# An FFN entry dealt out by granule, squares of the norms summed on GpSimd, decay floors computed in the first mixer

## The chip, the cores and the metric

The kernel runs on one core of a Trainium2 chip. The metric is the time of one execution on the device, in microseconds, lower is better. A core has five engines with a queue of instructions each: TensorE (PE in the profile, with its weight loads as PEld), VectorE (DVE), ScalarE (ACT), GpSimd (POOL) and SyncE (SP), which here issues most of the DMAs. Each engine works off its queue in order. An instruction waits until the ones that it depends on, on other engines, have signalled, and everything behind it in its queue waits with it.

## The reference

A trunk of two layers on x of 512 tokens by 1024 features, all in float32. Each layer has three sub-layers, each with a norm ahead and a residual sum behind:

```python
x = x + 1/2 * SwiGLU_a(RMSNorm(x))          # FFN1
h = RMSNorm(x) @ W_mix_in                   # one projection for three token mixers
y = concat[shortconv | HGRN2 | FoX]
x = x + y @ W_mix_out
x = x + 1/2 * SwiGLU_b(RMSNorm(x))          # FFN2
# rms_norm(x) = x * rsqrt(mean(x*x) + 1e-6) * gain
# swiglu(h)   = (silu(gate) * up) @ w_out,  [gate | up] = h @ w_in,  2816 hidden features
```

HGRN2 is a recurrence with decay; the lower bound of its decay ("floor") comes from a softmax and a cumulative sum over a table of 2 x 256 logits, which depends on nothing else.

## The kernel before, in words

x is held transposed, features on the partitions: eight tiles of 128 features x 512 tokens (`xT`). TensorE multiplies in float32 to full precision with three passes: each operand is split into a rounded high part `hi` and the rest `lo`, and hi·hi, hi·lo and lo·hi are summed (`mm3`, L322, matmuls at L327, L333, L334). So every weight needs a cast on ScalarE (hi) and a subtraction on VectorE (lo): `parted` for plain weights (L315, L316), `prepare` for the halved products (L696, L698). Both share three buffers (tag `hl`); a buffer comes free when the matmuls on it are done.

An FFN has 22 tiles of 128 hidden features, each with a gate and an up part. Its first matmuls can't wait for the norm, which needs all of x; so the first tiles are **covered**: they are multiplied from x times the gain, without the norm's factor `inv`, and corrected afterwards. Four tiles are covered in three of the FFNs, six in the first (the opening of the program). Two tiles make a pass, indexed by f, of four **granules**; one granule is two blocks of 128 rows of the weights (a load on SP of 2 x 256 KB, a cast, a subtraction, 24 matmuls of 128x512). So an entry has 8 granules, the opening 12.

The remaining tiles use a Strassen-like scheme: each pair of tiles is made of seven **products** P1, P2, P6, P5, P7, P3, P4, in this order, of half the contraction and half the tokens each (24 matmuls of 128x256 each). Their operands on the side of x come from the normalised x in four quarters (a, b): a is the half of the features, b the half of the tokens. `halves_of_x` (L578) computes the quarters with `inv` (L594, four instructions each), the four totals of quarters (L600), and the seven operands, each with a cast on ScalarE and a rest on VectorE (`two`, L624). On the weights' side `halved` (L636) loads four quarters of 512 KB (L749 for the first pair, L667 later), and sums them on VectorE (`total`, L684) or by accumulating DMAs that GpSimd issues (L671, L714). The seven results are collected in PSUM banks and copied out: P1, P6, P7 and P4 accumulate in turn in one bank, so that P6 waits for the copy g1 (L789) and P7 for the copy g2 (L796); P3 accumulates in P5's bank behind the copy u2 (L799). Weights are prepared three products ahead (LEAD).

What makes the order: the framework's scheduler places instructions by priority, except for those that `follow` (L276) chains, which stay in the order in which the program issues them on their engine. Before, the products' own work is chained; of the entry only the last pass's clearing is (below); the granules' casts and rests run at high priority, and the operands are placed by the scheduler.

**The norm.** While x's tiles are completed, `norm_part` writes hi and lo of x times gain, squares the tile on ScalarE (L414, buffer tag g2 with two buffers in an FFN, t with more in the mixers) and adds it to `sqacc` on VectorE (L415): seven adds for each of the six norms. `end_norm` sums over the partitions with a matmul against a constant matrix (L427), then takes Ln and Exp on ScalarE (behind a load of their table, L263) and one Newton step (`rsqrt`: Square on ScalarE, three operations on VectorE, L421 to L423) to get `inv`.

**Clearing.** `finish` takes a covered tile from its two banks: gate and up times `inv` (L554, L555), Silu (L270), and two hidden products of 128x256 (L573, L576). In passes before the last this follows the pass; for the last pass the first tile is finished after the first product and the second after the third.

**In the opening** x is loaded in pieces and transposed on TensorE (L1509), constants are built, and `lower_bounds` (L835) computes the decay floors: some 20 small operations on VectorE, two on ScalarE and a load of the logits.

Of the kernel before, what the change touches and what calls it, by code (L numbers as in the profile page):

```python
# [23 lines left out]
P = 128  # L24
T = 512
# [11 lines left out]
LEAD = 3  # L37

# [124 lines left out]
class Trunk:  # L163
# [119 lines left out]
    def granule(self, parts, kk, ahead=True, skew=0):  # L283
# [14 lines left out]
        with self.tc.high_priority() if ahead else ExitStack():  # L298
            hi, lo = self.parted(st[:, : kk * c], 1 if ahead else kk, skew)
# [3 lines left out]
    def parted(self, src, pieces=1, skew=0):  # L303
# [38 lines left out]
    def stream_steps(self, jobs, parts_of, act, nk, mid=None, pre=None):  # L342
# [10 lines left out]
        while k < nk:  # L353
# [6 lines left out]
            rows = self.granule(parts_of(k, kk), kk, pre is None, skew)  # L360
# [6 lines left out]
            for n, ((acc, cols, toks, *more), j) in enumerate(order):  # L367
                if pre is not None and n == len(order) // 2:
                    pre(k, True)
                if isinstance(mid, tuple) and (k, len(order) // 2) == (mid[0], n):  # L370
                    mid[1]()
# [3 lines left out]
                if toks is None:  # L375
                    self.mm3(acc, hi[:, cols], lo[:, cols], ah, al, first, last)
# [15 lines left out]
    def norm_part(self, j, pool, xj=None, part=None):  # L392
# [19 lines left out]
        else:  # L412
            sq = pool.tile([P, T], F32, tag=self.tt, name=self.n("sq"), bufs=self.tb)
            nc.scalar.activation(sq, xj, AF.Square)  # L414
            nc.vector.tensor_add(self.sqacc, self.sqacc, sq)  # L415

    def rsqrt(self, out, v, r, t):

        nc = self.nc
        self.act(t, r, AF.Square)  # L420
        nc.vector.scalar_tensor_tensor(out=t, in0=v, scalar=EPS, in1=t, op0=ALU.add, op1=ALU.mult)  # L421
        nc.vector.tensor_scalar(t, t, scalar1=-0.5, scalar2=1.5, op0=ALU.mult, op1=ALU.add)
        nc.vector.tensor_mul(out, r, t)  # L423

    def end_norm(self, bank, pool):
        nc = self.nc
        nc.tensor.matmul(bank, self.ones_mean, self.sqacc, start=True, stop=True)  # L427
# [3 lines left out]
        self.act(r, bank, AF.Ln, bias=self.epsc)  # L431
        self.act(r, r, AF.Exp, scale=-0.5)
        self.inv = self.res.tile([P, T], F32, tag="inv", name=self.n("inv"))
        self.rsqrt(self.inv, bank, r, t)


    def ffn(self, w_in, w_out, next_gain, covered, begin=None, out=None):
# [5 lines left out]
        with tc.tile_pool(name=self.n("ffn"), bufs=1) as fp:  # L443
            self.tt, self.tb = "g2", 2
            if begin is not None:
                x, gain, logits = begin
            self.hq = {}
            halved = self.halved(fp, w_in, w_out, covered)
            finish = self.cover(fp, w_in, covered, begin, halved)
            for n, _ in enumerate(halved):  # L450

                if n in (1, 3):
                    finish(n // 2)
# [42 lines left out]
    def cover(self, fp, w_in, covered, begin, then):  # L496

# [4 lines left out]
        if begin is not None:  # L502
            x, gain, logits = begin
        for f in range(0, covered, 2):
# [6 lines left out]
            opening = f == 0  # L511

            def norm():
                self.end_norm(self.bank("pt" if self.ntog % 2 == 0 else "po"), fp)
                self.xparts = self.halves_of_x(fp)

                for _ in range(2 if begin is not None else 7):
                    next(self.xparts)

# [3 lines left out]
                parts, self.xact, KD,  # L523
                (2, norm) if opening and begin is None else None,
                (lambda *a: self.open_x(x, gain, fp, *a)) if opening and begin else None,
            )
            if opening and begin is not None:
                nt = iter(["xh4", "xl4", "xh5", "xl5", "xh6", "xl6", "r2", "r3", "r4", "r5"])
                self.build_consts(lambda dt: fp.tile([P, T], dt, tag=next(nt), name=self.n("c")))
                self.lower_bounds(logits, fp.tile([P, T], F32, tag="g1", name=self.n("lb"), bufs=2))  # L530
                norm()
            if f == 2:
                for _ in self.xparts:
                    pass
            if f + 4 == covered or f + 2 == covered:
                next(then)
            if opening:
# [1025 lines left out]
```

## Time and profile before

| | us |
|---|---|
| median of 3 runs | 1864.13 (1862.87 to 1872.72) |
| profiled execution | 1866.59 |
| span of it in the trace | 1864.7 |
| PE busy | 1834.3 (98%) |
| DVE busy | 1482.1 (79%) |
| ACT busy | 1009.1 (54%) |
| POOL busy | 177.4 (10%) |

The mean clock that TensorE was granted is 0.996 of full speed. Roughly, by the trace: the first FFN runs to 347 us, the first mixer to 605, its FFN2's first granule starts at 605 and its first product at 649; the second layer's FFN1 starts at 939 with its first product at 983, its FFN2 at 1522 with the first product at 1567. A row of a timeline is: start, duration, engine, line, operation, out<-in with shapes, and in brackets how long the engine stood idle before and what released it. A row of the waits has the waiting engine and group, what it waited for, and total us, times, longest. A row of a group has the count, busy us, mean ns of one, and the idle time before. A row of a stretch has its length, the busy time and count of the engine, the granted clock (PEclk), the share of the DMA engines and GB/s.

### The profile page before, as it was taken

Reading aid. Unit: us, or ns where it says so; the run is one execution under the profiler, and the core shown is the slowest. Engines: PE = TensorE matmul, PEld = TensorE weight load, DVE = VectorE, ACT = ScalarE, POOL = GpSimd, SP = SyncE. Lnnn points to the kernel's source line nnn. Section 1 sums busy time; section 2 is a strip of 40 time slices with the busy share of each in tenths; the row PEclk is TensorE's granted clock in tenths of the full one; section 3 lists DMA queues with packets and bytes.
Section 4 is the critical chain, followed back from the end, with each engine's and each line's share of the span. In section 5 each row is a group of like instructions: output and inputs, shape, how many; then the busy total and the mean of one; then the engine's idle time right before and its main releaser. Section 6 shows DMA issues by size and latency. Waiting matters only on the chain.

```text
span 1864.7 us, 33370 instructions
## 1 busy us (share of the span) xinstructions
PE 1834.3 (98%) x13528; PEld 1705.3 (91%) x13528; DVE 1482.1 (79%) x2101; ACT 1009.1 (54%) x1467; POOL 177.4 (10%) x182
## 2 busy tenths in 40 slices
PE   8999999999999999999999999999999999999999
PEld 6899999899878799999989999988998787999997
DVE  7889886678887978879687887967868878888883
ACT  4455554564666545555454555545547654555552
POOL 0011120100000011112001111201000000021210
PEclk9999999999999999999999999999999999999999
DMA  7658783232222757878265797813323237577662
GB/s 203 169 119 191 180 180 92 71 94 70 74 79 92 218 109 168 188 178 170 74 198 133 162 193 181 170 63 92 79 60 90 80 106 205 143 158 198 148 136 91
DMA packets 245418, 251.91 MB, mean 135 GB/s; under 512 B 19568, under 2 KB 230000, under 8 KB 245264
## 3 DMA queue, kind: packets, MB, share of 16 engines
q1 hardware_dynamic: 191664, 183.69, 32.9%
q0 software_dynamic: 53600, 66.09, 22.2%
q8 instruction: 106, 1.74, 0.4%
q14 instruction: 48, 0.39, 0.1%
HBM read 223.98 MB, written 2.10 MB: 121 GB/s over the span
## 4 chain that ended last, share of the span: by engine, by line
PE 85%; DVE 8%; ACT 3%; issue 2%; DMA 2%; SPq 0%; ACTq 0%; DVEq 0%
PE mm L327 12%; PE mm L334 12%; PE mm L333 12%; PE sc L334 6%; PE sc L327 6%; PE sc L333 6%; PE pt L327 6%; PE pt L333 6%; PE pt L334 6%; PE po L327 3%; PE po L334 3%; PE po L333 3%; DVE hl L316 1%; ACT hl L315 1%; PE po L1412 1%
## 5 line engine op out<-in xcount | busy, mean ns | idle before, releaser
L696 ACT CAST hl<-w 128x1024 fp32r<-128x1024 f32 x322 | 337.4, 1049 | 337.2 <-PE mm L334 76.6
L698 DVE TENSOR_TENSOR hl<-w,hl 128x1024 fp32r<-128x1024 f32 x322 | 393.0, 1222 | 102.5 <-ACT hl L696 102.5
L316 DVE TENSOR_TENSOR hl<-st,hl 128x512 fp32r<-128x512 f32 (+2 forms) x196 | 166.7, 852 | 117.0 <-ACT hl L315 115.9
L315 ACT CAST hl<-st 128x512 fp32r<-128x512 f32 (+2 forms) x196 | 146.6, 750 | 189.0 <-PE mm L334 66.9
L327 PE MATMUL mm<-xc,hl 128*128 128x256 f32 (+1 forms) x730 | 201.4, 276 | 1.1 <-ACT g L796 1.1
L334 PE MATMUL mm<-xc,hl 128*128 128x256 f32 x728 | 201.3, 276 | 0.0
L333 PE MATMUL mm<-xc,hl 128*128 128x256 f32 x728 | 201.2, 276 | 0.0
L334 PE MATMUL sc<-xc,hl 128*128 128x256 f32 x528 | 148.6, 281 | 8.7 <-DVE hl L698 8.7
L327 PE MATMUL sc<-xc,hl 128*128 128x256 f32 (+1 forms) x530 | 148.3, 281 | 0.9 <-ACT g L796 0.9
L333 PE MATMUL sc<-xc,hl 128*128 128x256 f32 x528 | 148.0, 280 | 0.0
L327 PEld LDWEIGHTS mm<-xc,hl 128*128 128x128 f32 x730 | 137.0, 188 | 1.6 <-ACT g L796 1.5
L333 PEld LDWEIGHTS mm<-xc,hl 128*128 128x128 f32 x728 | 136.7, 188 | 0.0
L334 PEld LDWEIGHTS mm<-xc,hl 128*128 128x128 f32 x728 | 136.6, 188 | 0.1
L327 PE MATMUL pt<-xc,hl 128*128 128x256 f32 x480 | 132.6, 276 | 0.0
L333 PE MATMUL pt<-xc,hl 128*128 128x256 f32 x480 | 132.6, 276 | 0.0
L334 PE MATMUL pt<-xc,hl 128*128 128x256 f32 x480 | 132.6, 276 | 0.0
L327 PE MATMUL mm<-hl,x 128*128 128x256 f32 (+1 forms) x384 | 112.6, 293 | 0.7 <-DVE ft L421 0.4
L334 PEld LDWEIGHTS sc<-xc,hl 128*128 128x128 f32 x528 | 101.3, 192 | 9.2 <-DVE hl L698 9.1
L327 PE MATMUL mm<-x,hl 128*128 128x512 f32 x272 | 109.6, 403 | 0.0
L334 PE MATMUL mm<-hl,x 128*128 128x256 f32 (+1 forms) x384 | 107.7, 281 | 0.0
L333 PE MATMUL mm<-hl,x 128*128 128x256 f32 (+1 forms) x384 | 107.5, 280 | 0.0
L334 PE MATMUL mm<-x,hl 128*128 128x512 f32 x272 | 106.5, 392 | 0.0
(470 smaller groups left out, 5693.3 us busy)
## 6 DMA issues: line engine op xcount, KB each, us to landing
w<-in_ffn_w_in_dram SPq DMA_DIRECT2D x140, 512.0 KB, 5.3
w<-in_ffn_w_out_dram SPq DMA_DIRECT2D x64, 512.0 KB, 4.4
w<-in_ffn_w_out_dram POOLq DMA_DIRECT2D x56, 512.0 KB, 9.1
st<-in_w_mix_in_dram SPq DMA_DIRECT2D x88, 256.0 KB, 2.7
st<-in_ffn_w_in_dram SPq DMA_DIRECT2D x72, 256.0 KB, 3.3
w<-in_ffn_w_in_dram POOLq DMA_DIRECT2D x35, 512.0 KB, 8.2
w<-S POOLq DMA_DIRECT2D x35, 512.0 KB, 4.7
st<-in_ffn_w_out_dram SPq DMA_DIRECT2D x24, 512.0 KB, 3.7
```

The lines of the kernel that those rows point to most:

```text
L315: a = nc.scalar.copy(hi, src[:, c : c + w])
L316: b = nc.vector.tensor_sub(lo, src[:, c : c + w], hi)
L327: i = nc.tensor.matmul(acc[:, c], ah, bh[:, c], start=first and c.start == 0, stop=False, skip_group_check=True,)
L333: nc.tensor.matmul(acc, ah, bl, start=False, stop=False, skip_group_check=True)
L334: i = nc.tensor.matmul(acc, al, bh, start=False, stop=last, skip_group_check=True)
L696: A(nc.scalar.copy(hi, src))
L698: return lambda: V(nc.vector.tensor_sub(lo, src, hi))
L1412: nc.tensor.matmul(self.ob[:, t0 + u * P : t0 + 2 * P], V[:, j, h % 4].rearrange("p a d -> p (a d)"), part[:, j, u:, :].rearrange("p i t - ...
```

## The change

Four things, in one diff:

1. A table `ENTRY` says for each granule (counted from 0; each half of a granule can be named; from twice the number of covered tiles on, the numbers count products) what is dealt there: the sum of squares over the partitions ("squares"), the rest of the norm ("norm"), a normalised quarter ("x a b"), a total of quarters ("+ a b c d": quarter (a, b) += quarter (c, d)), an operand ("P1"), the first total of weights ("sum"), the correction and Silu of a tile ("clear t") and its hidden products ("values t"). `deal` issues them, and chains all of them. `finish` and `halves_of_x` are gone. The granules of an entry are chained too and lose their high priority. With four covered tiles the norm's sum stands at 2.5 granules; it stood at 1.5 in the second layer's FFN1 and at 3 in the FFN2s. All operands except P3 and P4 and the first two tiles stand ahead of the first product, the rest between the products. The loads of the first products' weights (`halved`) are issued with the entry's first pass done.
2. The adds of `norm_part` go from VectorE to GpSimd.
3. `ngain` (minus the gain) is computed on VectorE instead of ScalarE.
4. `lower_bounds` is called in the first layer's mixer, behind the norm of its input.

In the queues as the changed kernel is built, the operand P4 and the total "0 0 += 1 0" stand on both engines ahead of the copy g2 that product P7 waits for, and on SP the four loads of the first products in FFN2 stand ahead of granule 4's loads, where they stood behind granule 6's.

```diff
+ENTRY = {
+    4: {
+        2.5: "squares", 5: "norm, x 0 0", 6: "P1, x 1 0", 7: "x 0 1, + 0 0 0 1, P2", 8: "P5, x 1 1",
+        9: "clear 0, + 0 0 1 1", 10: "P6, sum, clear 1, values 0, values 1, + 0 1 1 1, P7",
+        11: "P3", 12: "clear 2, values 2, + 0 0 1 0, P4", 14: "clear 3, values 3",
+    },
+    6: {
+        7: "norm, x 0 0", 8: "x 1 0, clear 0, clear 1", 9: "x 0 1, P1, + 0 0 0 1",
+        10: "P2, values 0, values 1, x 1 1", 11: "P5, clear 2, + 0 0 1 1", 12: "P6, values 2, sum, clear 3",
+        13: "values 3, + 0 1 1 1, P7", 14: "P3", 15: "+ 0 0 1 0, P4", 16: "clear 4, values 4",
+        18: "clear 5, values 5",
+    },
+}
...
-        with self.tc.high_priority() if ahead else ExitStack():
-            hi, lo = self.parted(st[:, : kk * c], 1 if ahead else kk, skew)
+        with self.tc.high_priority() if ahead and not keep else ExitStack():
+            hi, lo = self.parted(st[:, : kk * c], 1 if ahead else kk, skew, keep)
...
-            if pieces > 1:
+            if pieces > 1 or keep:
                 self.follow("a", a)
                 self.follow("v", b)
...
+            if deal is not None:
+                deal(k)
...
-                if isinstance(mid, tuple) and (k, len(order) // 2) == (mid[0], n):
-                    mid[1]()
+                if deal is not None and n == len(order) // 2:
+                    deal(k + 1)
...
             nc.scalar.activation(sq, xj, AF.Square)
-            nc.vector.tensor_add(self.sqacc, self.sqacc, sq)
+            nc.gpsimd.tensor_add(self.sqacc, self.sqacc, sq)
...
+        def clear(t):
+            gi = fp.tile([P, T], F32, tag="g2", name=self.n("gi"), bufs=2)
+            ui = fp.tile([P, T], F32, tag="u2", name=self.n("ui"), bufs=2)
+            pg, pu = tiles[t]
+            V(nc.vector.tensor_mul(gi, pg, self.inv))
+            V(nc.vector.tensor_mul(ui, pu, self.inv))
+            A(self.act(gi, gi, AF.Silu))
+            values[t] = gi, ui
+
+        def deal(n):
+            for what in filter(None, ENTRY[covered].get(n, "").split(", ")):
+                name, *at = what.split()
+                at = [int(v) if v.isdigit() else v for v in at]
+                if what == "squares":
+                    squares()
+                elif name == "norm":
+                    for e, i in self.take_norm(norm[0], fp):
+                        self.follow(e, i)
+                    self.table(SILU)
+                    self.signs()
+                elif name == "x":
+                    self.normalise(fp, *at)
+                elif name == "+":
+                    x, y = (self.xn[tuple(v)] for v in (at[:2], at[2:]))
+                    V(nc.vector.tensor_add(x, x, y))
...
+                else:
+                    self.operand(fp, name)
...
+            if f + 4 == covered:
+                next(halved)
+        for _ in halved:
+            pass
...
-        yield
-        total(u, "S2")
-        for s in seq[: LEAD - 1]:
-            prepare(*s)()
-        run(-1)
-        yield
-        prepare(*seq[LEAD - 1])()
+        for n, s in enumerate(seq[:LEAD]):
+            deal(2 * covered + n)
+            prepare(*s)()
+        run(-1)
...
             run(n)
-            yield
+            deal(2 * covered + LEAD + n)
...
                 bz = features([(H_F, 256)], ("mm", "mm"), lambda: self.end_norm(self.bank("pt"), hp))
+                if l == 0:
+                    self.lower_bounds(logits, hp.tile([P, T], F32, tag="t", name=self.n("lb"), bufs=8))
                 bg = features([(H_G, 256)], ("mm", "po"))
```

More of the change, by code (lines that the diff above doesn't have):

```diff
@@ L280, in follow, with granule @@
         self.chain[engine] = i.ins.name
[L283 removed]
+    def granule(self, parts, kk, ahead=True, skew=0, keep=False):
         nc = self.nc
@@ L445, in ffn @@
             if begin is not None:
-                x, gain, logits = begin
+                x, gain = begin
             self.hq = {}
[L448 to L453, printed above, removed]
+            self.cover(fp, w_in, w_out, covered, begin)
             f0, nf = CHUNKS[-1]
@@ L509, in parts @@
                 return [w_in[r, f * P : (f + 2) * P], w_in[r, FF + f * P : FF + (f + 2) * P]]
[L511 to L518, printed above, removed]
+            opening = f == 0 and begin is not None
             self.stream(
                 [(bk, slice(c, c + P), None) for bk, c in zip(banks, (0, 256, 128, 384))],
-                parts, self.xact, KD,
-                (2, norm) if opening and begin is None else None,
-                (lambda *a: self.open_x(x, gain, fp, *a)) if opening and begin else None,
-            )
@@ L532, in cover @@
[L532 to L537, printed above, removed]
[L538 to L559 removed]
+                squares()
```

153 lines of the change are left out of this document (77 added, 76 removed).

## The prediction

> **What bounds the kernel now.** I read first the page's busy shares, then what TensorE waits for, then the rows around its longest wait, then the groups by shape. Head of the page:
>
> ```profile
> span 1864.7 us, 33370 instructions
> PE 1834.3 (98%) x13528; PEld 1705.3 (91%) x13528; DVE 1482.1 (79%) x2101; ACT 1009.1 (54%) x1467; POOL 177.4 (10%) x182
> ```
>
> TensorE is busy for 98% of the span, so only a stall of TensorE, or its clock, can change the time. Its waits (total us, times, longest us):
>
> ```profile
> PE sc L334 <- DVE hl L698: 8.7, 2, 4.4
> PE mm L1509 <- DMA xs<-in_x_dram: 7.0, 2, 3.9
> ...
> PE po L327 <- DVE nt L421: 1.4, 1, 1.4
> PE mm L327 <- ACT g L796: 1.1, 2, 0.5
> PE sc L327 <- DVE gi L554: 1.1, 1, 1.1
> PE sc L327 <- ACT g L796: 0.9, 2, 0.5
> ```
>
> The change can reach all but the second (the load of x). The largest, 4.4 us, comes once in each FFN2, at the first halved product (TensorE's rows: start, duration):
>
> ```profile
> 649.47 0.33 PE L327 MATMUL sc<-xc,hl 128*128 128x128 f32 x2
> 649.64 0.33 PE L333 MATMUL sc<-xc,hl 128*128 128x256 f32 x1
> 654.33 0.58 PE L334 MATMUL sc<-xc,hl 128*128 128x256 f32 x1 [4.36 <-DVE hl L698]
> ```
>
> From issue to issue that is 4.7 us, 4.6 over the cadence. By stretches (length, PE busy, PEclk, DMA), the clock falls behind it:
>
> ```profile
> 645.00:650.00 5.00, 4.97 (x24) 1.00 0.38 112
> 650.00:655.00 5.00, 0.68 (x3) 0.70 0.66 210
> 655.00:660.00 5.00, 5.00 (x30) 0.62 0.58 105
> 660.00:665.00 5.00, 5.00 (x46) 1.00 0.72 105
> ```
>
> A clock of 0.70 over 5 us is 3.0 us at half clock, of which 0.7 us lie behind 654.33; 0.62 is 3.8 us more. So 6.8 us at half clock, 4.5 of them in work: 2.2 us lost. An FFN2 entry therefore loses 4.6 + 2.2, 0.5 at a later product (L796), and about 0.35 at the norm's sum (next fence): 7.6 us.
>
> ```profile
>   DVE sqa L415: 0.7, 2
> ```
>
> **The change, part by part.** The prices (group, busy, mean ns):
>
> ```profile
> L698 DVE TENSOR_TENSOR hl<-w,hl 128x1024 fp32r<-128x1024 f32 x322 | 393.0, 1222 | 102.5 <-ACT hl L696 102.5
> L684 DVE TENSOR_TENSOR w<-S,w 128x1024 f32<-128x1024 f32 x35 | 42.7, 1219 | 0.0
> L415 DVE TENSOR_TENSOR sqa<-sqa,sq 128x512 f32<-128x512 f32 x42 | 28.8, 685 | 0.0
> L600 DVE TENSOR_TENSOR xn<-xn,xn 128x1024 f32<-128x1024 f32 x16 | 19.3, 1220 | 0.0
> L634 DVE TENSOR_TENSOR xc<-xn,xc 128x1024 fp32r<-128x1024 f32 x16 | 19.1, 1220 | 0.0
> L573 DVE SCALAR_TENSOR_TENSOR hq<-gi,ui 128x256 f32<-128x256 f32 x18 | 7.6, 420 | 0.6 <-ACT gi L270 0.5
> L696 ACT CAST hl<-w 128x1024 fp32r<-128x1024 f32 x322 | 337.4, 1049 | 337.2 <-PE mm L334 76.6 <-PE pt L334 65.2 <-PE sc L334 58.2
> L270 ACT ACTIVATE gi<-gi 128x512 f32<-128x512 f32 x18 | 11.4, 632 | 15.1 <-DVE gi L554 15.1
> L796 ACT ACTIVATE g<-mm 128x512 f32<-128x512 f32 x13 | 7.7, 589 | 0.0
> ```
>
> Back to back they start closer together, as these rows of VectorE show:
>
> ```profile
> 643.63 0.69 DVE L554 TENSOR_TENSOR gi<-sc,inv 128x512 f32<-128x512 f32 x1
> 644.23 1.22 DVE L630 SCALAR_TENSOR_TENSOR xc<-xn,xc 128x1024 fp32r<-128x1024 f32 x1
> 645.37 1.22 DVE L634 TENSOR_TENSOR xc<-xn,xc 128x1024 fp32r<-128x1024 f32 x1
> ```
>
> So a 1024-column operation of VectorE occupies 1.14 us, a 512-column one 0.60; two hidden products of 256, 0.68. TensorE's clockwork shows in two casts that wait for the ends of granules 6 and 7 of the third FFN (rows of ScalarE):
>
> ```profile
> 977.78 1.05 ACT L696 CAST hl<-w 128x1024 fp32r<-128x1024 f32 x1 [0.53 <-PE pt L334]
> 983.22 1.05 ACT L696 CAST hl<-S 128x1024 fp32r<-128x1024 f32 x1 [4.39 <-PE pt L334]
> ```
>
> A granule lasts 983.22 − 977.78 = 5.44 us; a product, the same 24 matmuls on half the columns, 2.72.
>
> *The entry with four covered tiles (both FFN2s, second layer's FFN1).* The table takes the second tiles' clearing and hidden products from between the operands, so VectorE reaches the first product's weights early and the 4.6 us stall goes. What is late next is read from the queues as the changed kernel is built. The second product's weights (P2) use the buffer of granule 6, so their cast can't start before its end; everything in the given order stands behind them. I add from that end. Cast of P2's weights 1.05; on VectorE in this order: rest of P2's weights, operand P6, total S, clear of tile 1 (2 × 0.60), values of tiles 0 and 1 (2 × 0.68), addition 0 1 += 1 1, operand P7, weights of P6 and P5, total S3, operand P3, g1's subtraction (0.60), weights of P7, clear of tile 2 (1.20), values 2 (0.68), addition 0 0 += 1 0. Of these, eleven have 1024 columns (the rests of four weights, three operands, two totals, two additions): 11 × 1.14 = 12.5. Operand P7 waits for its own cast behind the addition, 1.05 + 0.15 = 1.2; values 2 wait for their Silu, 0.8. On ScalarE operand P4's cast follows that last addition (1.0), then P3's weights (0.95), and only then the copy g2 (0.6), which the fifth product, P7, needs because it accumulates into g2's bank. With 0.2 for the ends: 1.05 + 12.5 + 2.4 + 2.04 + 1.2 + 0.6 + 0.8 + 1.0 + 0.95 + 0.6 + 0.2 = 23.3 us. P7 is due after granule 7 and four products, 5.44 + 4 × 2.72 = 16.3. **TensorE stalls 7.0 us in each such entry**, about 1.1 at P6 (g1's copy stands behind operand P7's cast) and 5.9 at P7. Before, P4's operand was done ahead of the products and this copy was only 0.5 late. A 5.9 us idle is longer than the one behind which half clock lasted 6.8 us. That began about 2.4 us into the idle; so 3.5 us of it fall into the idle, 3.3 into work: 1.6 us lost.
>
> Second layer's FFN1: 7.0 + 1.6 − 0.5 (row L796 mm) = **+8.1**. Each FFN2: 7.0 + 1.6 − 7.6 = +1.0, **+2.0** in both.
>
> *The entry with six tiles (opening).* The norm's end stood behind the floors' logarithm on ScalarE, which leaves:
>
> ```profile
> 41.93 0.20 ACT L270 ACTIVATE lb<-lb 128x4 f32<-128x4 f32 x1 [3.05 <-DVE lb L885]
> ```
>
> It moves ahead by these 3 us, and f=0's banks are cleared at granule 8: the waits on nt and gi, 1.6 + 1.2 with what TensorE lost around them, go. But the addition 0 0 += 1 0 (1.14) and P4's operand (1.05 + 0.1 for its cast, 1.14) now stand between S3 and g1's subtraction, on the chain from the first product's end to g2's copy:
>
> ```profile
> 86.37 1.05 ACT L696 CAST hl<-w 128x1024 fp32r<-128x1024 f32 x1 [1.79 <-PE mm L334]
> 87.32 0.59 ACT L789 ACTIVATE g<-mm 128x512 f32<-128x512 f32 x1
> ...
> 94.34 0.58 ACT L796 ACTIVATE g<-mm 128x512 f32<-128x512 f32 x1
> ```
>
> It was 0.5 late (8.5 us from the cast at 86.37) and becomes 3.4 longer: a stall of 3.9. Stalls: −2.8 + 3.4 = +0.6. 3.9 is nearer to the 4.6 that cost clock than to the 1.4 and 1.1 that didn't; I take 2.0 for it: **+2.6**, ends −2.8 and +3.
>
> *Squares on GpSimd.* 42 adds of 0.685 us leave VectorE (28.8 us). The trace has no elementwise add on GpSimd. Its 182 instructions average 177.4 / 182 = 1.0 us, VectorE's add takes 0.69: I take 1.0 (it is GpSimd's own), ends 0.69 and 2.2, the latter over three times VectorE's. With two square buffers in an FFN, ScalarE's next square waits for the add before last. In the mixers the sum has room:
>
> ```profile
> 351.71 0.69 DVE L415 TENSOR_TENSOR sqa<-sqa,sq 128x512 f32<-128x512 f32 x1
> ...
> 354.93 1.02 PE L427 MATMUL pt<-sqa,ones_mean 128*128 128x512 f32 x2
> ```
>
> 2.5 us between. In FFN2 the last add at 1.0 comes before its sum (which also moves to 2.5 granules; in the second layer's FFN1 that is 5.4 us later, hidden by the clearing dealt behind it). Adds of 1.0 cost nothing; at 2.2 the Squares hold up the casts of the entry: +6 us in each FFN2. In the opening the adds stand on GpSimd behind an accumulating DMA (first row), but the last square ends at 34.3 (second) and the sum follows at 35.83, 1.5 later:
>
> ```profile
> 16.92 1.44 POOL L671 DMA_DIRECT2D w<-in_ffn_w_in_dram  x1 [15.27 <-DMA w<-in_ffn_w_in_dram]
> ```
>
> ```profile
> 33.73 0.60 ACT L414 ACTIVATE sq<-po 128x512 f32<-128x512 f32 x1 [2.34 <-DVE xT L1498]
> ```
>
> ```profile
> 35.83 1.06 PE L427 MATMUL po<-sqa,ones_mean 128*128 128x512 f32 x2
> ```
>
> So 1.0 is hidden there as well. The Trainium skill, "GPSIMD Engine Reference", section 3.1 (Elementwise), measures an fp32 add at 1.96 times VectorE's; an estimate from it is 1.34 us, and the sum would be 0.2 us higher in each FFN2. No run here shows it yet.
>
> *Loads on SP.* The four 512 KB loads of the first products go ahead of granule 4's in FFN2 and wait for GpSimd's last add: 0 while they land within 8 us, up to +3 each if 10. *Decay floors*: some 20 small VectorE operations of about this row's 0.1 us each, two on ScalarE and one load go to the first mixer:
>
> ```profile
> 40.05 0.23 DVE L863 TENSOR_TENSOR lb<-lb 128x2 f32<-128x2 f32 x2
> ```
>
> 2 us beside products whose weights lie two granules ahead: 0, at most +1. *ngain* on VectorE is one such operation, hidden.
>
> **Sum:** +8.1 + 2.0 + 2.6 = +12.7 on the profiled execution, 1866.6 (1864.7 of span and 1.9 around it), which lies 2.5 above the median, 1864.1. In medians: **1876.8 us**; own range 1868 to 1884.
>
> On the clock I weighed a rule. The trace shows half clock behind each 4.6 us idle and none behind 1.4 or less. The Trainium skill, "TensorE: Matmul & The Clock Gate", Part 1 (The HAM clock gate), puts the change to half rate after an idle free-running window of some 3.4 us. By it 3.9 and 5.9 us idles may but need not hold a whole window: the sum would lie between +5.9 and +12.7. The trace bears on it only through the two idles of 4.6, both followed by half clock.
>
> **Rivals.** (A) *Slow squares*: GpSimd's adds near 2.2 us, or the loads late: twice +6 → about 1889. For: nothing in the trace bounds them; against: 1.0 us for its other work. (B) *The delay splits*: VectorE and ScalarE gain some 3 us on the sum of 23.3 (waits overlap), each four-tile entry stalls 4.0, too short for half clock: FFN1 +3.5, FFN2s 2 × (4.0 − 7.6), opening −1.5 → −5, 1859: within 0.5%. (C) *The other side*: the copy g2 isn't late. If P4's operand were ready by the fourth product, all entry losses go: 2 × 7.6 + 2.8 + 0.5 + 0.5 = −19 → 1845. It decides at the 16.3 us: the chain must be shorter by 7. Against it: its terms are measured durations in a fixed order. For it: between granules 4 and 6 VectorE runs further ahead than before, and an operation that I count behind P2's weights would have to run ahead of them. (D) *The change doesn't do what it says* (the queues as built deviate on the chip): excluded by the given order, so no chance of its own.
>
> **Chances.** Forecast 0.52, A 0.10, B 0.18, C 0.20. A measurement of this kernel tells a difference of about 0.5% (9.3 us) from none. Forecast and A are slower by more (1873.5 on; the forecast's lower tail lies inside, as much as B's upper lies out): slower 0.61, within 0.5% 0.18, faster 0.21. The range leaves out C's full gain and the far tail of A: 1851 to 1888.
>
> **What would show it.** First products of FFN2: no wait on VectorE (L732, the weights' rest). Fifth product of every four-tile entry: a wait of some 6 us on ScalarE's copy g2, and behind it a clock near 0.5 for some us; 3.9 in the opening. GpSimd's adds near 1 us and no wait at the sums. I am wrong if the fifth product waits under 2 us, or if the fifth's wait exists but the sums or the granules wait as well.

## The result, and the profile after

The changed kernel takes 1896.14 us (median of 4 runs, 1891.26 to 1902.74) against 1864.53 before: a ratio of 1.0159, 95% interval 1.0131 to 1.0188. It is slower, as forecast, but by 31.6 us instead of 12.7, and outside the range. The profiled execution took 1902.74 us, the longest of the four. Line numbers from here on are those of each run's own kernel; the matmuls of `mm3` are L345, L351 and L352 in the changed one. The head of its page:

```profile
span 1901.0 us, 33370 instructions
## 1 busy us (share of the span) xinstructions
PE 1853.1 (97%) x13528; PEld 1721.7 (91%) x13528; DVE 1487.6 (78%) x2063; ACT 1006.9 (53%) x1462; POOL 246.5 (13%) x224
```

VectorE issues 38 instructions fewer and is yet 5.5 us longer busy; TensorE does the same matmuls in 18.8 us more. Its waits (total, times, longest):

```profile
PE mm L345 <- ACT g L829: 8.5, 2, 5.1
PE sc L352 <- DVE hl L334: 7.3, 5, 2.5
PE sc L345 <- ACT g L829: 7.2, 2, 3.6
PE mm L1544 <- DMA xs<-in_x_dram: 7.1, 2, 3.9
PE sc L345 <- ACT g L822: 4.6, 2, 2.4
...
PE mm L345 <- ACT g L822: 1.4, 1, 1.4
```

The first product's 8.7 us on VectorE's rests are gone. In their place come 15.7 us for the copy g2 (L829, four times, at the fifth product), 6.0 for g1 (L822, at the third product), and 7.3 for rests of the granules (L334), for which before no granule waited.

Where the time went is seen by laying the two traces side by side, the n-th matmul of one against the n-th of the other. The changed one is late, in us: 5.0 when the opening's fifth granule starts, 2.9 at its first product, 8.6 behind the half clock that follows the wait at its fifth product, 15.7 at the end of that FFN; 15.4 at the start of FFN2, 22.8 twenty microseconds into its products and to its end; 31.3 behind the entry of the second layer's FFN1; 31.0 and 36.9 before and behind the last entry; 36.2 at the end. So the opening costs 8.6, the rest of the first FFN 7.1, the FFN2 entries 7.4 and 5.9, the FFN1 entry 8.5; the mixers give back 0.6 and the end of the last FFN 0.7.

The fifth product of the second layer's FFN1, the one the prediction worked out, on TensorE and then on ScalarE:

```profile
1012.87 0.38 PE L345 MATMUL mm<-xc,hl 128*128 128x256 f32 x1 [1.36 <-ACT g L822]
1023.74 0.58 PE L345 MATMUL mm<-xc,hl 128*128 128x256 f32 x1 [5.15 <-ACT g L829]
```

```profile
1021.21 1.06 ACT L663 ACTIVATE xc<-xn 128x1024 fp32r<-128x1024 f32 x1 [1.97 <-DVE xn L572]
1022.17 1.03 ACT L730 CAST hl<-w 128x1024 fp32r<-128x1024 f32 x1
1023.10 0.59 ACT L829 ACTIVATE g<-mm 128x512 f32<-128x512 f32 x1
```

Operand P4's cast (L663) waits for the total 0 0 += 1 0 (L572), P3's weights follow, then the copy. That is the chain of the prediction, 1.36 + 5.15 = 6.51 us of waits against 7.0.

What it didn't foresee shows in three groups: the adds on GpSimd, and VectorE's rows beside them, of before and then of after (min, median, max ns).

```profile
L436 POOL TENSOR_TENSOR sqa<-sqa,sq x42: 1292/1623/2164, 17.7 to 1563.0; 128x512 f32<-128x512 f32 x42
```

```profile
L401 DVE SCALAR_TENSOR_TENSOR x<-xT,gain,x x40: 741/746/753, 328.9 to 1537.1; 128x512 fp32r<-128x512 f32 x40
```

```profile
L422 DVE SCALAR_TENSOR_TENSOR x<-xT,gain,x x40: 734/1183/1778, 344.7 to 1563.4; 128x512 fp32r<-128x512 f32 x40
```

An add takes 1.62 us in the median and 1.29 at the least, not 1.0, and the same VectorE instruction beside it 1.18 instead of 0.75. In the opening, VectorE and then GpSimd:

```profile
16.26 0.75 DVE L422 SCALAR_TENSOR_TENSOR x<-po,gain,x 128x512 fp32r<-128x512 f32 x1 [3.21 <-ACT x L421]
16.93 4.82 DVE L334 TENSOR_TENSOR hl<-st,hl 128x512 fp32r<-128x512 f32 x2
21.67 0.68 DVE L1533 COPY xT<-po 128x512 f32<-128x512 f32 x1
```

```profile
17.69 3.51 POOL L436 TENSOR_TENSOR sqa<-sqa,sq 128x512 f32<-128x512 f32 x2
```

Two rests of 0.68 us take 4.82: the second ends half a microsecond behind two adds that run from 17.69 to 21.20. A granule waits for it.

And one thing of TensorE itself, in the first FFN's products: 20 us stretches of before, then of after (length, PE busy and count, PEclk):

```profile
130.00:150.00 20.00, 20.00 (x179) 1.00 0.86 167
150.00:170.00 20.00, 20.00 (x179) 1.00 0.89 176
```

```profile
130.00:150.00 20.00, 20.00 (x172) 1.00 0.59 120
150.00:170.00 20.00, 20.00 (x173) 1.00 0.79 175
```

At a granted clock of 1.00 and without a wait, TensorE issues a matmul every 117.8 ns instead of 113.3, by the mean step from start to start in these stretches (the expectations below call it 117.5 and 113). That lasts from about 107 us, behind the fifth product's stall and its half clock, to the end of the FFN, and is the 7.1 us above.

### The profile page after: what moved, and what is told of

Read it like the earlier page. It is cut to its first block, busy times and chain, and to the rows that moved or that the text cites. A ratio compares the mean times of both kernels' runs of the same rounds, so it can differ in the third digit from the quotient of the medians.

```text
span 1901.0 us, 33370 instructions
## 1 busy us (share of the span) xinstructions
PE 1853.1 (97%) x13528; PEld 1721.7 (91%) x13528; DVE 1487.6 (78%) x2063; ACT 1006.9 (53%) x1462; POOL 246.5 (13%) x224
## 4 chain that ended last, share of the span: by engine, by line
PE 80%; DVE 10%; ACT 4%; DMA 2%; issue 2%; POOL 1%; SPq 1%; ACTq 0%; DVEq 0%; POOLq 0%
PE mm L345 12%; PE mm L352 12%; PE mm L351 12%; PE sc L345 5%; PE sc L352 5%; PE sc L351 5%; PE pt L345 5%; PE pt L351 5%; PE pt L352 5%; PE po L345 3%; PE po L351 3%; PE po L352 3%; DVE hl L334 2%; DMA st<-in_ffn_w_in_dram 1%; DVE xn L641 1%
## 5 line engine op out<-in xcount | busy, mean ns | idle before, releaser
L334 DVE TENSOR_TENSOR hl<-st,hl 128x512 fp32r<-128x512 f32 (+2 forms) x196 | 174.4, 891 | 138.6 <-ACT hl L333 137.7
L345 PE MATMUL mm<-xc,hl 128*128 128x256 f32 (+1 forms) x730 | 205.4, 282 | 9.8 <-ACT g L829 8.5
L352 PE MATMUL mm<-xc,hl 128*128 128x256 f32 x728 | 204.8, 281 | 0.0
L351 PE MATMUL mm<-xc,hl 128*128 128x256 f32 x728 | 204.8, 281 | 0.0
L345 PE MATMUL sc<-xc,hl 128*128 128x256 f32 (+1 forms) x530 | 150.3, 284 | 11.8 <-ACT g L829 7.2
L352 PE MATMUL sc<-xc,hl 128*128 128x256 f32 x528 | 149.7, 283 | 0.0
L351 PE MATMUL sc<-xc,hl 128*128 128x256 f32 x528 | 149.6, 283 | 0.0
L345 PEld LDWEIGHTS mm<-xc,hl 128*128 128x128 f32 x730 | 139.5, 191 | 10.6 <-ACT g L829 8.9
L352 PEld LDWEIGHTS mm<-xc,hl 128*128 128x128 f32 x728 | 140.2, 193 | 0.0
L351 PEld LDWEIGHTS mm<-xc,hl 128*128 128x128 f32 x728 | 139.1, 191 | 0.0
L345 PE MATMUL pt<-xc,hl 128*128 128x256 f32 x480 | 133.1, 277 | 0.0
L351 PE MATMUL pt<-xc,hl 128*128 128x256 f32 x480 | 132.9, 277 | 0.0
L352 PE MATMUL pt<-xc,hl 128*128 128x256 f32 x480 | 132.8, 277 | 0.0
L748 POOL DMA_DIRECT2D w<-S x35 | 31.1, 888 | 662.5 <-DVE hl L732 481.6
L345 PEld LDWEIGHTS sc<-xc,hl 128*128 128x128 f32 x530 | 103.2, 195 | 12.7 <-ACT g L829 7.6
L345 PE MATMUL mm<-hl,x 128*128 128x256 f32 (+1 forms) x384 | 112.3, 292 | 0.7 <-DVE qk L1374 0.3
L345 PE MATMUL mm<-x,hl 128*128 128x512 f32 x272 | 109.8, 404 | 0.0
L352 PE MATMUL mm<-hl,x 128*128 128x256 f32 (+1 forms) x384 | 107.4, 280 | 0.0
L351 PE MATMUL mm<-hl,x 128*128 128x256 f32 (+1 forms) x384 | 107.1, 279 | 0.0
```

Source lines behind the costliest of these rows:

```text
L345: i = nc.tensor.matmul(acc[:, c], ah, bh[:, c], start=first and c.start == 0, stop=False, skip_group_check=True,)
L351: nc.tensor.matmul(acc, ah, bl, start=False, stop=False, skip_group_check=True)
L352: i = nc.tensor.matmul(acc, al, bh, start=False, stop=last, skip_group_check=True)
L748: G(nc.gpsimd.dma_start(raw[u, 1], sums[u], accum_op=ALU.add))
```

## The experiments

Theories at the start: **T1**, while a GpSimd add runs, VectorE can't work on two SBUF operands; rival **T2**, the adds are only slow and late. A third is that the dealt order delays the granules by itself. Later, on TensorE's slower cadence: **T3**, a wait long enough to bring half clock brings it; **T4**, the place in the order of the work decides it. "Before" is measured anew with each set, 1863.6 to 1865.6.

**Adds on VectorE, the rest of the change kept**

```diff
-            nc.gpsimd.tensor_add(self.sqacc, self.sqacc, sq)
+            nc.vector.tensor_add(self.sqacc, self.sqacc, sq)
```

> The changed kernel with the 42 adds of the squares back on VectorE; table, floors and ngain stay. Both theories below hold the adds on GpSimd for the part of the loss that the prediction missed. By either, the 5 us that the opening loses before its fourth granule, the 2.6 us at granule 1 of each FFN2 with the clock behind it, and the 2.4 us at each FFN2's third product mostly go; the fifth product's wait stays, 4 to 6 us in every entry. So 10 to 16 us faster than the changed kernel, near 1882, and still 12 to 20 slower than the kernel before. A third theory, that the dealt order itself delays the granules, expects the same waits at the granules as in the changed kernel and under 4 us of gain.

1902.54 us (1890.12 to 1912.23), ratio to before 1.0165 (1.0113 to 1.0217): no gain. The opening did gain: its fifth granule starts 0.7 us ahead of before instead of 5.0 behind, its first product 3.0 ahead instead of 2.9 behind. But FFN2's granule 1 still waits:

```profile
PE sc L345 <- ACT g L829: 10.1, 2, 5.1
PE mm L345 <- ACT g L829: 8.5, 2, 5.2
...
PE sc L352 <- DVE hl L334: 6.1, 2, 3.1
```

So there the third theory holds as well: the granule's rest stands in the given order behind 12 us of other VectorE work. And in this profile three FFNs ran at 117.8 ns, against one in the changed kernel's: that ate the rest.

**Only the adds on GpSimd, in the kernel before**

```diff
-            nc.vector.tensor_add(self.sqacc, self.sqacc, sq)
+            nc.gpsimd.tensor_add(self.sqacc, self.sqacc, sq)
```

> The kernel before with nothing changed but the engine of the 42 adds: GpSimd. Theory T1 (while a GpSimd add of some 1.6 us runs, VectorE can't start or finish an operation on two SBUF operands): VectorE rows of 2 to 5 us for 512 columns beside the adds, granules that wait for VectorE's rests in the opening and at FFN2's granule 1, 10 to 16 us slower than before. Theory T2 (the adds are only slow and come late to the squares' two buffers and to the sum): VectorE's rows keep their 0.7 us, waits at the sums and at the granules behind ScalarE's squares, 3 to 8 us slower.

1876.66 us (1874.57 to 1885.26), ratio 1.0047 (1.0025 to 1.0069); median to median +11.1.

```profile
PE po L427 <- POOL sqa L415: 10.8, 3, 5.2
...
PE mm L334 <- DVE hl L698: 4.3, 1, 4.3
```

Both theories show: the sums wait for GpSimd (T2), and VectorE's row is as long as in the changed kernel (T1):

```profile
L401 DVE SCALAR_TENSOR_TENSOR x<-xT,gain,x x40: 732/1198/1850, 332.0 to 1547.4; 128x512 fp32r<-128x512 f32 x40
```

In both FFN2s the late sum only takes the place of the first product's wait; in the second layer's FFN1 the first product now waits 4.3 us, where it had not.

**The adds where they were, and a GpSimd add beside each**

```diff
             nc.vector.tensor_add(self.sqacc, self.sqacc, sq)
+            same = self.xT[:, j, :]
+            nc.gpsimd.tensor_add(same, same, self.zero[:, 0:1].to_broadcast([P, T]))
```

> The kernel before, its adds on VectorE as they were, and beside each of them a GpSimd add of the same shape that nothing waits for soon: x's tile plus a zero column, in place, so that the values stay. T1: the same long VectorE rows beside these adds as with the adds moved, and 6 to 16 us slower than before, although no square and no sum waits for GpSimd. T2: the time of before within 3 us, VectorE's rows unchanged.

1877.03 us (1875.08 to 1893.16), ratio 1.0068 (1.0045 to 1.0091); +11.4, though nothing waits for these adds. VectorE is busy for 1506.8 us, 24.7 more than before, with one instruction more; its own adds to the sum come late by that, and TensorE waits for them:

```profile
PE po L431 <- DVE sqa L417: 7.8, 3, 3.5
```

T1 is shown. VectorE and GpSimd at FFN2's entry:

```profile
612.50 1.53 DVE L403 SCALAR_TENSOR_TENSOR x<-xT,gain,x 128x512 fp32r<-128x512 f32 x1
613.95 0.68 DVE L417 TENSOR_TENSOR sqa<-sqa,sq 128x512 f32<-128x512 f32 x1
614.55 1.87 DVE L1056 TENSOR_TENSOR xT<-mm,xT 128x512 f32<-128x512 f32 x3
```

```profile
612.12 1.36 POOL L419 TENSOR_TENSOR xT<-xT,zero 128x512 f32<-128x512 f32 x1 [1.89 <-DVE x L403]
614.17 1.35 POOL L419 TENSOR_TENSOR xT<-xT,zero 128x512 f32<-128x512 f32 x1 [0.69 <-DVE x L403]
```

The first row, two SBUF operands, starts inside an add and ends 0.55 us behind its end (613.48). The three additions at 614.55 take one operand from PSUM; they run through the second add at 0.6 us each. The Trainium skill, "SBUF — State Buffer", section "SBUF: two separate sides", says it so: a VectorE operation with two SBUF inputs and a GpSimd operation that reads SBUF take one port pair in turn, the later one blocked for the whole instruction. The rows agree on the whole: an operation blocked to the add's very end would end 0.75 us behind it, but spans on GpSimd are rough.

**Operand P4 and the later clearing behind the copy g2**

```diff
-        11: "P3", 12: "clear 2, values 2, + 0 0 1 0, P4", 14: "clear 3, values 3",
+        11: "P3", 13: "+ 0 0 1 0, P4", 14: "clear 2, values 2", 16: "clear 3, values 3",
...
-        13: "values 3, + 0 1 1 1, P7", 14: "P3", 15: "+ 0 0 1 0, P4", 16: "clear 4, values 4",
-        18: "clear 5, values 5",
+        13: "values 3, + 0 1 1 1, P7", 14: "P3", 17: "+ 0 0 1 0, P4", 18: "clear 4, values 4",
+        20: "clear 5, values 5",
```

> The changed kernel with one thing changed in the table: the total 0 0 += 1 0, operand P4 and the clearing of the later tiles are dealt after the copy g2 (two products later). The prediction's step (the fifth product waits because g2's copy stands behind operand P4 on ScalarE): the wait at the fifth product falls from 3.5 to 5.3 us to under 2 in all four entries and the half clock behind it goes, 8 to 16 us faster than the changed kernel, near 1884; the waits at the granules stay. If something else holds the fifth product (the weights of P7, say), the wait stays above 3 us and the time within 4 us of the changed kernel.

1901.85 us (1892.53 to 1911.29), ratio 1.0184 (1.0136 to 1.0231): no gain, although the waits for g2 did what the step says. None over 0.4 us is left in any entry. In the second layer's FFN1 0.7 us each stand at the sixth and seventh product instead; in the first FFN2 the third product now waits longer for g1, 4.1 us. The FFN1's rows, then the FFN2's:

```profile
1003.96 0.48 PE L345 MATMUL mm<-xc,hl 128*128 128x256 f32 x1 [1.85 <-ACT g L822]
1014.67 0.39 PE L345 MATMUL mm<-xc,hl 128*128 128x256 f32 x1 [0.66 <-ACT u L832]
1018.30 0.39 PE L345 MATMUL mm<-xc,hl 128*128 128x256 f32 x1 [0.63 <-DVE u L835]
```

```profile
664.98 0.39 PE L345 MATMUL sc<-xc,hl 128*128 128x256 f32 x1 [4.07 <-ACT g L822]
```

The FFN1 entry costs 4.8 us by the side-by-side count, not 8.5. But three FFNs ran their products at 117.8 ns (x172 in a 20 us stretch at clock 1.00), which costs 7 to 9 us each.

**The table alone**: adds on VectorE, granules out of the given order and at high priority again

```diff
-            rows = self.granule(parts_of(k, kk), kk, pre is None, skew, deal is not None)
+            rows = self.granule(parts_of(k, kk), kk, pre is None, skew)
```

> The changed kernel with the adds on VectorE and the granules' casts and rests back at high priority and out of the given order; what is left is the table of operands, clearing and values, and the floors in the mixer. If the 3.2 us wait at FFN2's granule 1 that is left without GpSimd's adds comes from the granules' place in the given order, it goes, and the time (runs without the slower cadence) is 8 to 10 us below that of the changed kernel with adds on VectorE; the fifth product's waits of 3.5 to 5.3 us stay. If it comes from elsewhere it stays.

1885.03 us (1882.23 to 1891.87), ratio 1.0090 (1.0059 to 1.0121).

```profile
PE sc L345 <- ACT g L829: 9.9, 2, 5.0
PE mm L345 <- ACT g L829: 8.5, 2, 5.2
...
PE po L455 <- DVE sqa L436: 4.9, 2, 2.4
```

The granules' waits are gone; the sum at 2.5 granules now waits 2.4 us in each FFN2, which replaces most of it. The fifth product's waits stay.

**The same with P4 late**

```diff
-        11: "P3", 12: "clear 2, values 2, + 0 0 1 0, P4", 14: "clear 3, values 3",
+        11: "P3", 13: "+ 0 0 1 0, P4", 14: "clear 2, values 2", 16: "clear 3, values 3",
...
-        13: "values 3, + 0 1 1 1, P7", 14: "P3", 15: "+ 0 0 1 0, P4", 16: "clear 4, values 4",
-        18: "clear 5, values 5",
+        13: "values 3, + 0 1 1 1, P7", 14: "P3", 17: "+ 0 0 1 0, P4", 18: "clear 4, values 4",
+        20: "clear 5, values 5",
```

> The changed kernel with three things undone or moved: adds on VectorE, granules out of the given order and at high priority, operand P4 and the later tiles' clearing behind the copy g2. If these three are all that the table costs, its waits at the fifth products (3.5 to 5.3 us) fall to under 1 us and 20 to 24 us go against the same kernel without the third: 1860 to 1866, about the time of before; the wait for the norm's sum at 2.5 granules (2.6 us in each FFN2) stays. If the table costs something else, it stays above 1872.

1890.87 us (1883.20 to 1892.48), ratio 1.0103 (1.0052 to 1.0155): the time missed. The waits didn't: 0.4 us at most for g2 and 1.4 elsewhere, but for the sum's 2.4 and the load of x. The trace has 7014 steps of 116 to 119 ns from matmul to matmul, 4.4 ns too long each, 30.9 us; the trace of before has 1542, 6.8 us. Without that difference it would lie at 1892.2 − 24.1 = 1868.1.

**The same count for the other traces** parts the slower cadence from what the edits do. It is one profile each, spans in us:

| kernel | span | steps of 116 to 119 ns | span less 4.4 ns for each, against before |
|---|---|---|---|
| before | 1864.7 | 1542 | 0 |
| changed | 1901.0 | 2842 | +30.6 |
| changed, second profile (below) | 1898.5 | 2888 | +27.9 |
| changed, adds on VectorE | 1910.4 | 6744 | +22.8 |
| table alone | 1889.9 | 3126 | +18.2 |
| table, P4 late | 1890.1 | 7014 | +1.3 |
| changed, P4 late | 1899.7 | 6704 | +12.3 |

So the adds on GpSimd cost the changed kernel 5 to 8 us, the granules' place in the given order 4.6, and P4 and the clearing ahead of g2 16.9 (16 to 18 by the first and the last rows). The two profiles of the changed kernel lie 2.7 apart, which says how far such differences can be trusted.

**Does a stall bring the slower cadence?** The kernel before, the copy g2 repeated

```diff
-                A(nc.scalar.activation(g2, acc, AF.Copy, scale=-1.0))
+                for _ in range((1, 7, 10, 13, 16, 19, 9, 15, 21)[(w - covered) // 2]):
+                    A(nc.scalar.activation(g2, acc, AF.Copy, scale=-1.0))
```

> The kernel before with the copy g2 repeated on ScalarE in each pair of tiles (1, 7, 10, 13, 16, 19, 9, 15, 21 times), which makes the fifth product wait some 1 to 9 us, 34 times, and changes no value. It asks what a stall among products costs beside itself. Theory T3: TensorE's cadence in the products (113 ns from matmul to matmul) has a second state of 117.5 ns that only a spell of half clock can leave behind, by chance: behind waits under 3 us neither comes, behind waits over 4 us half clock comes each time and the cadence behind it is 117.5 ns in some cases and 113 in others, until the next spell. Rival T4: the second state belongs to the changed kernel's order of instructions (the same products are always slow) and comes or goes without half clock.

One run, 2059.93 us. The cadence changed some 15 times, each time behind a gap or a spell of half clock, to the slower as to the faster. T3 falls in its condition: 117.8 ns came behind a 1.9 us wait without half clock, and behind 5.7 and 9.0 us ones with it; 3.6 and 3.0 us ones ended it; most waits changed nothing.

**The changed kernel, a second profile**: no edit

> The changed kernel itself, a second profile. In its first profile the first FFN ran its products at 117.5 ns from the wait at the fifth product on, the other three at 113. If the slower cadence is drawn by chance at the waits, another set of FFNs is slow this time, with the same instructions, and the times lie in steps of some 7 to 9 us from about 1888 up. If it belongs to the order of the instructions, the first FFN is slow again and only it.

1904.09 us (1890.26 to 1908.87). The first FFN runs slow again, behind the same wait, from 104 us, and no other but for some 5 us in the last and the last 28 us of the third:

```profile
95.00:100.00 5.00, 1.67 (x15) 1.00 0.01 4
100.00:105.00 5.00, 5.00 (x32) 0.66 0.00 0
130.00:150.00 20.00, 20.00 (x172) 1.00 0.64 127
700.00:720.00 20.00, 20.00 (x179) 1.00 0.69 163
```

That speaks for T4, the order, in this place; the four times, 19 us apart, speak for chance elsewhere. So does the second layer's FFN1: behind the same wait of 5.15 us at its fifth product it ran slow with the adds on VectorE, and, but for its end, fast in both profiles of the changed kernel. It is not settled.

**Floors alone**, in the kernel before

```diff
-                self.lower_bounds(logits, fp.tile([P, T], F32, tag="g1", name=self.n("lb"), bufs=2))
...
+                if l == 0:
+                    self.lower_bounds(logits, hp.tile([P, T], F32, tag="t", name=self.n("lb"), bufs=8))
```

> The kernel before with the floors in the first mixer and nothing else. If the prediction's step holds (the norm's end waits for the floors' logarithm), the waits of 1.4 and 1.1 us in the opening go and the mixer is not later: 2 to 3 us faster than before among runs without the slower cadence. If the floors delay the mixer, no gain.

1861.25 us (1858.81 to 1871.07), ratio 0.9963 (0.9934 to 0.9993). The first product of the opening is 2.4 us ahead of before, the wait on gi is gone, that on nt is 0.4 us instead of 1.4, and the mixer gives nothing back.

**The first product's wait, taken away with less.** The kernel before; operands P7 and P4 are chained and issued behind the first products, the total of weights behind the first two casts, the last tiles cleared later

```diff
+            if name in ("P7", "P4"):
+                self.follow("a", i[0]), self.follow("v", i[1])
...
-        add((0, 0), (1, 0))
         yield part("P7")
+        yield self.follow("v", add((0, 0), (1, 0)))
         yield part("P4")
...
-                if n in (1, 3):
-                    finish(n // 2)
+                if n < 3:
+                    next(self.xparts)
+                if n in (3, 6):
+                    finish(n // 6)
...
-        total(u, "S2")
         for s in seq[: LEAD - 1]:
             prepare(*s)()
+        total(u, "S2")
         run(-1)
```

> The kernel before, adds on VectorE, no table: only the operands P7 and P4 (with the total between them) and the first total of weights are issued behind the first product's weights, and the last pass's tiles are cleared behind the copy g2. Theory: the first product of FFN2 waits 4.6 us because of 3.4 us of operands and 1.1 us of a total that it doesn't need; moved behind it they hide beside the products if they stay off the chain to g2's copy. Then the waits of 4.4 us go to under 0.5, the 0.5 us ones at the fifth product go in all four entries, no half clock follows, and no FFN2 falls into the slower cadence: 14 to 18 us faster than before, near 1849, without the second group of times 8 to 9 us above. Rival: the work moved stalls the third or fifth product instead, as in the changed kernel, and the time is within 5 us of before.

1860.75 us (1852.45 to 1876.97), ratio 0.9977 (0.9946 to 1.0009). The 4.4 us waits and the half clock are gone; each FFN2 entry gains 7.3 us. Waits of 0.6 to 0.7 us stay behind the clearing, and the slower cadence follows in some FFNs: times near 1852, 1861, 1869 and 1877. The gain in the median is not clear of the noise.

**With the floors**: the edits of the last two runs together

```diff
-                if n in (1, 3):
-                    finish(n // 2)
+                if n < 3:
+                    next(self.xparts)
+                if n in (3, 6):
+                    finish(n // 6)
...
-                self.lower_bounds(logits, fp.tile([P, T], F32, tag="g1", name=self.n("lb"), bufs=2))
```

> The same with the decay floors computed in the first mixer, as in the change. If the norm's end in the opening waits for the floors' logarithm, the waits of 1.4 and 1.1 us there go: 2 to 3 us faster than the run above, near 1846. If the floors delay the mixer, the mixer gives back as much.

1859.06 us (1850.42 to 1859.80), ratio 0.9944 (0.9923 to 0.9964); three of nine runs near 1851, six near 1859.

**The clearing later still**

```diff
-                if n in (3, 6):
-                    finish(n // 6)
+                if n in (4, 7):
+                    finish(n // 7)
```

> The light edit with the floors, and the last pass's two tiles cleared later still: the first behind product P7, the second behind the next pair's P1. Theory: in the light edit the 0.8 us waits at the seventh product (behind u2's addition, which stands behind the first clearing on VectorE) and at the next pair's third product (behind g1's copy, which stands behind the second tile's Silu on ScalarE) put TensorE into the slower cadence by chance. Without these waits the group of times near 1859 thins out and most runs lie at 1848 to 1851. Rival: the slower cadence comes without a wait, and the two groups stay as they were.

1854.02 us (1847.88 to 1857.87), ratio 0.9921 (0.9882 to 0.9959): the lowest median of all, 10 us below before and 42 below the changed kernel, though its interval overlaps that of the run above. Half of the runs still lie near 1857.

**Its Silu moved as well**: the second tile's clearing in two parts, behind P4 and behind the next g1

```diff
-                if n in (4, 7):
-                    finish(n // 7)
+                if n == 4:
+                    for _ in finish(0):
+                        pass
+                if n == 6:
+                    tile = finish(1)
+                    next(tile)
+                if n == 7:
+                    next(tile, None)
...
         V(nc.vector.tensor_mul(ui, pu, self.inv))
+        yield
         A(self.act(gi, gi, AF.Silu))
```

> The light edit with the floors; the first of the last pass's tiles is cleared behind product P7, the second in two parts, its products with the norm's factor behind P4 and its Silu behind the next pair's g1. If the 0.6 to 0.9 us wait for the next pair's g2 in the run before (its copy stood behind that Silu) is only a matter of place, it goes, and with fewer waits fewer runs fall into the slower cadence: median under 1851, nearly all runs between 1846 and 1851. If the slower cadence comes regardless of the waits, a third of the runs stay 8 us above.

1864.80 us (1856.79 to 1872.52), ratio 0.9998 (0.9973 to 1.0022). The waits for g2 went from 0.8 and 0.5 us to 0.2 and the time rose: in the profile one FFN2 goes slow at its first product, at a gap of a single matmul's length, and stays so to its end. The kernel above goes slow at the same gap and comes back at a later one, 20 us on. Fewer gaps may also mean fewer occasions to come back; that is not shown. The expectation, that fewer waits bring less of it, fell.

## Why the prediction was wrong

**The step that failed is "Adds of 1.0 cost nothing".** The size was off (1.62 us in the median; the prediction's other estimate, 1.34, lies near the least, 1.29), and the mechanism was missing: the add blocks VectorE. The prediction held the adds against the sums and against ScalarE's squares, and not against what runs on VectorE at the same time. Alone that costs 11 us (shown by the adds beside, for which nothing waits). In the changed kernel it costs 5 to 8 us by the count above, and 5.0 of them are what the opening loses before its fifth granule. The granules' 2.5 us in each FFN2 stay without it: with the adds on VectorE they are 3.1.

**Failed with it: "In FFN2 the last add at 1.0 comes before its sum".** In the table alone the adds are VectorE's own, of 0.68 us, and the sum at 2.5 granules still waits 2.4 us in each FFN2. In the changed kernel this is hidden, because a granule ahead of it waits already.

**Not priced at all:** that the granules lose their high priority. The change says so, and the prediction follows the given order only from granule 6 on. With the adds on VectorE the granule's rest is 3.1 us late; with the priority back it isn't. So the FFN2 entries cost 7.4 and 5.9, not +1.0 each: 2.5 at the granule were missing and, in the first of them, 1.6 of clock behind it; the third product waited 2.2 and 2.4 instead of 1.1, and the fifth 3.6, less than the 5.9 (5.2 and 5.0 in the second profile). It is what the prediction named last among its signs of being wrong: the fifth's wait exists, and the granules wait as well.

**The fifth product: right, and the largest cost.** 5.15 + 1.36 us against 5.9 + 1.1 in the second layer's FFN1, +8.5 in all against +8.1. In the opening 3.3 against 3.9. Taking P4 and the clearing behind g2 removed it, with 17 us by the count above, which shows the chain; the two were not moved apart. That the change is slower was therefore forecast for its main reason and not by luck. The clock: 3.3 us of idle brought half clock, as taken; in the opening it cost 2.7 instead of 2.0.

**The floors and the norm: right.** −2.4 against −2.8.

**Outside the model:** the slower cadence, 7.1 us in the first FFN of the profiled execution, and 5.7 over the whole span against before (12.5 against 6.8). Every time in the prediction assumes 113 ns. It would also explain why before's runs lie at 1863 to 1867 and again at 1872 to 1875, as 13 and 5 of 18 did. Without the slower cadence the parts add up: 12.7 forecast, 5 to 8 for the adds, 4.6 for the granules' order and 4.9 for the two sums are 27 to 30 us, where the two profiles show 28 to 31.

Of the rivals, (A), slow squares, came nearest, 1889 with a chance of 0.10; but its mechanism, squares that hold up casts in each FFN2, is not what cost most: there the granules waited for their place in the order. That its time lies near the measured one is luck.

## What to carry to other kernels

Work moved to an idle engine isn't free if it shares a port with the busy one: look at what the busy engine runs in the same microseconds, and which of its operands lie in SBUF. An order written out by hand fixes what stands ahead of what; follow it for every instruction that it newly binds, from its first one, and not only from the one that was late. And when a stall is removed, a smaller edit that only moves the work that the waiting product doesn't need (two operands and a total) gained 7 us per FFN2 entry, where the full table lost as much.

## What the runs showed of the hardware

TensorE's products run at one of two cadences, 113.3 or 117.8 ns for 128x256, both at a granted clock of 1.00. In the traces read for it, a change from one to the other lies behind a gap, sometimes of one matmul's length, and the cadence then holds to some later gap, for up to 240 us. What decides which one follows is open: neither the length of the wait nor half clock does, and one place came out slow twice.

Half clock came behind shorter idles than the 4.6 us of before: in the changed kernel's FFN2 behind 2.2 us.

```profile
676.98 0.58 PE L345 MATMUL sc<-xc,hl 128*128 128x256 f32 x1 [2.21 <-ACT g L822]
```

```profile
670.00:675.00 5.00, 4.77 (x43) 1.00 1.06 285
675.00:680.00 5.00, 3.02 (x14) 0.69 0.76 125
```

In the kernel with repeated copies waits of 2.0 to 3.0 us brought it in five cases of eight, those of 3.6 and more always, those under 2 never. Elsewhere the bounds blur: the changed kernel with P4 late has it behind 1.85 us (the row at 1003.96 above), and the kernel with an add beside each has none behind 3.55. In these traces each spell of half clock, but for the one that the end of the program cuts short, lasts 3.4, 6.8 or 10.2 us.
